# Loading the neighbourhood values by image rows of all four blocks instead of by blocks: a two-layer hybrid attention kernel

## The chip, the cores and the metric

One core of a Trainium2 chip runs the whole program. The metric is the time that the device takes for one execution, in microseconds (us). The core has a matrix engine (TensorE, in the profile PE, with PEld for its weight loads), VectorE (DVE), ScalarE (ACT), GpSimd (POOL) and SyncE (SP). SP computes nothing; it issues transfers between the device's memory and the on-chip memory, one after the other in the program's order. The transfers run on 16 DMA engines. The on-chip memory has 128 rows, called partitions.

## The reference

The model has two post-norm layers over 1024 latent tokens (an image of 16 rows of 64 columns) and 256 context tokens, 1024 wide, in float32. The change lies in the first layer's token mixer. It has four differential attention heads and eight neighbourhood heads of width 64. A neighbourhood head lets each latent token look at a window of 8 rows and 16 columns around it and at all context tokens:

```
row_start = jnp.clip(r - wr // 2, 0, rows - wr)
col_start = jnp.clip(cidx - wc // 2, 0, GRID_W - wc)
...
bias = rpb[:, roff[:, None, None], col_off[None, :, :]]
s_win = jnp.einsum('bhqd,bhqkd->bhqk', q_row, k_win).astype(jnp.float32) * scale + bias
s_ctx = jnp.einsum('bhqd,bhkd->bhqk', q_row, k_ctx).astype(jnp.float32) * scale
p = jax.nn.softmax(jnp.concatenate([s_win, s_ctx], -1), axis=-1).astype(v.dtype)
return (jnp.einsum('bhqk,bhqkd->bhqd', p[..., :nw], v_win)
        + jnp.einsum('bhqk,bhkd->bhqd', p[..., nw:], v_ctx))
```

Around it stand the input and output projections, a second attention layer of another kind, and two feed-forward blocks, which the change does not touch.

## The kernel before

The program runs its stages in order: the first projection (`qkv`, which writes queries, keys and values to device memory), the first attention (`attn0`), the output projection and feed-forward of layer 0, the second layer's attention, and its feed-forward. All run on one core.

`attn0` works through eight units: units 0 to 3 are the differential heads, units 4 to 7 two neighbourhood heads each. A neighbourhood unit has nine jobs: one for the context tokens, then, for each of four groups j of 16 image columns and each of the two heads (hh), one job. A job's queries are 256 tokens (16 rows by 16 columns, in two halves s); its keys are 16 image rows of a band of 32 columns that begins at c0 = 0, 8, 24 or 32. The 512 window keys are four blocks of 128: block rb holds image rows 4 rb to 4 rb + 3, 32 columns each.

A job is cut into steps, and a table by hand (`PATTERN`, line 42) says how many rounds after the job's start each step is recorded, one job starting per round. For neighbourhood jobs: scores (X), their maximum with the bias table added (TR, on VectorE, line 943), the exponentials (E), two memsets on GpSimd that blank the unused part (MS, lines 952 and 953, three rounds on), the scaling by the reciprocal of the sum (S, GpSimd, line 820, two rounds on), transposes (T4 and T2, PE, line 830), a split into two summands, the products with the values (A, PE, five rounds on), and the output (FC, FIN, VectorE line 998, five rounds on). Order within PE, ACT, DVE and POOL is the order of recording, and nothing overtakes.

Between the jobs, `na_hooks` (line 1101) records what is fetched: values by `na_values` (line 1007), bias tables by `na_table` (line 1021), and the add of the mask to a table by `na_mask` (line 1028, on GpSimd). Values of group 0 and four of the six tables of a unit are asked for during the last jobs of the unit before; the mask add of its first table is recorded before its last job. The queries and keys of the next unit (`attn_unit`: twelve loads `ks`, `qs`, `ql`) are asked for before the fourth job. All these go out on SP's one queue, in this order, together with the store of a finished unit (line 1002). Each transfer there also waits until the eighth one before it has landed, since eight completion counters are used in turn.

The values lie in device memory as `svb`, 1280 tokens by 8 heads by two summands by 64, that is 4 KB for each token; a unit's two heads take 1 KB of them. A tile `vs` (128 partitions, four blocks, two heads, 128 numbers) holds one group j; seven such tiles are used in turn. The partition of a key in its block is 32 times the row in the block plus the column in the band. Tables (`tab`) are loaded by a pair of transfers each, with a source whose outermost count is 8.

Of the kernel before, what the change touches and what calls it, by code (L numbers as in the profile page):

```python
# [80 lines left out]
class Kernel:  # L81
# [925 lines left out]
    def na_values(self, sb, u, j):  # L1007

        src = self.svb[:, (u - 4) * 2:(u - 3) * 2].rearrange("t h a d -> t (h a d)")
        if j < 0:  # L1010
            v = self.vs[u, "c"] = self.t(sb, [P, 2, 2, P], "vc", F32R, bufs=2)
            self.dma(v.rearrange("p t h d -> p t (h d)"), src[NX:T, :].rearrange("(t p) c -> p t c", p=P))
        else:
            c0 = (0, 8, 24, 32)[j]
            v = self.vs[u, j] = self.t(sb, [P, 4, 2, P], "vs", F32R, bufs=7)
            for rb in range(4):
                sr = src[rb * 256 + c0:rb * 256 + c0 + 1, :]
                self.dma(v[:, rb].rearrange("p h d -> p (h d)"),
                         bass.AP(sr.tensor, sr.offset, [[64 * 1024, 4], [1024, 32], [1, 256]]))

    def na_table(self, sb, u, hh, v):

# [1783 lines left out]
```

## Time and profile before

| | us |
|---|---|
| median of three timed runs | 3321.28 |
| lowest, highest | 3315.80, 3325.24 |
| profiled execution | 3321.84 |
| its span | 3320.1 |
| PE busy | 3053.2 |
| VectorE busy | 2430.5 |
| ScalarE busy | 1547.6 |
| GpSimd busy | 981.9 |

The busy times are of the whole span; stages with different limits lie behind them. The neighbourhood units take the stretch from about 620 to 890 us. Views of the trace can be asked for a stretch: the waits (which instruction of which engine waited for what), the instructions in order of time, and the busy time of each engine with the granted TensorE clock (1.00 is 2.4 GHz, 0.50 is 1.2 GHz), the mean busy share of the 16 DMA engines and the rate that they moved.

### The profile page before, as it was taken

The page shows a single profiled execution, that of the slowest core. Times are in us where ns is not written, and L with a number is a line of the kernel's source. Part 1 is how long each engine was busy: PE and PEld are TensorE (multiplying, and loading weights), DVE is VectorE, ACT ScalarE, POOL GpSimd, SP SyncE. Part 2 cuts the span into 40 slices and gives each one's busy share as a digit, 9 for nine tenths or more (in the row PEclk, how much of TensorE's full clock was granted, in tenths as well). Part 3 has the DMA queues.
Part 4 walks back from the last instruction along what each step waited for, and adds up shares of the span by engine and source line. Part 5 has one row for each costly group of instructions (what it writes and reads, how often), then busy time and mean ns, then how long its engine had stood idle before and what let it go on. Part 6 is the DMA issues. An engine that isn't in the chain of part 4 may idle for free.

```text
span 3320.1 us, 47807 instructions
## 1 busy us (share of the span) xinstructions
PE 3053.2 (92%) x17519; PEld 2708.8 (82%) x17519; DVE 2430.5 (73%) x4109; ACT 1547.6 (47%) x3186; POOL 981.9 (30%) x772
## 2 busy tenths in 40 slices
PE   7999989975888899889999999989999899999996
PEld 5999878874777899679999788768998788888875
DVE  5776669875778998588998654448887876665576
ACT  5344357775634444333544336137774433333443
POOL 1345445563543321131231002123543101111021
PEclk9999999997998999999999999989999999999998
DMA  7565564375524333644342444264423322225542
GB/s 229 160 214 192 174 173 104 96 170 152 166 82 134 108 115 102 178 144 123 108 140 89 150 154 170 89 221 117 96 69 111 108 83 83 89 81 182 179 134 89
DMA packets 369191, 444.67 MB, mean 134 GB/s; under 512 B 52430, under 2 KB 265071, under 8 KB 365499
## 3 DMA queue, kind: packets, MB, share of 16 engines
q1 hardware_dynamic: 367629, 438.44, 43.8%
q8 instruction: 138, 2.26, 0.3%
q0 software_dynamic: 848, 3.02, 0.3%
q14 instruction: 96, 0.79, 0.1%
q10 hardware_dynamic: 480, 0.16, 0.0%
HBM read 344.51 MB, written 98.18 MB: 133 GB/s over the span
## 4 chain that ended last, share of the span: by engine, by line
PE 43%; DVE 9%; issue 3%; ACT 2%; DMA 2%; POOL 0%; SPq 0%; ACTq 0%; DVEq 0%; POOLq 0%
PE pa L125 18%; PE pc L125 17%; PE xps L125 3%; DVE blk L1736 2%; PE ops L125 2%; PE b L830 2%; DVE big L1830 1%; PE b L125 1%; ACT eu L1327 1%; DVE big L2246 0%; DMA eh<-hm 0%; DVE pt L1835 0%; ACT blk L1733 0%; DVE eu L1414 0%; DVE r L1259 0%
## 5 line engine op out<-in xcount | busy, mean ns | idle before, releaser
L125 PE MATMUL pc<-u,blk 128*128 128x320 f32 (+1 forms) x3540 | 631.6, 335 | 24.3 <-DVE blk L1736 10.1
L125 PEld LDWEIGHTS pc<-u,blk 128*128 128x128 f32 x3540 | 571.3, 191 | 66.1 <-DVE blk L1736 12.5
L1733 ACT CAST blk<-big 128x512 fp32r<-128x512 f32 x311 | 190.1, 621 | 301.5 <-PE pc L125 115.1
L125 PE MATMUL pa<-blk,blk 128*128 128x512 f32 x1188 | 291.5, 396 | 18.8 <-DVE blk L1736 16.4
L1736 DVE TENSOR_TENSOR blk<-wf,blk 128x512 fp32r<-128x512 f32 x377 | 290.1, 772 | 7.1 <-ACT blk L1733 7.1
L125 PEld LDWEIGHTS pa<-blk,blk 128*128 128x128 f32 x1188 | 225.6, 191 | 73.0 <-issue 9.2
L1733 ACT CAST blk<-wf 128x512 fp32r<-128x512 f32 x377 | 232.1, 618 | 111.4 <-PE pc L125 59.8
L1736 DVE TENSOR_TENSOR blk<-big,blk 128x512 fp32r<-128x512 f32 x311 | 224.3, 721 | 57.7 <-ACT blk L1733 57.6
L125 PE MATMUL pa<-u,blk 128*128 128x320 f32 (+1 forms) x1356 | 241.3, 327 | 9.2 <-DVE pt L1835 8.3
L125 PE MATMUL ps<-uh,whl 128*128 128x320 f32 (+2 forms) x1024 | 233.8, 315 | 8.6 <-DVE whl L122 5.9
L125 PEld LDWEIGHTS pa<-u,blk 128*128 128x128 f32 x1356 | 215.5, 190 | 20.5 <-DVE pt L1835 9.0
L125 PE MATMUL pc<-blk,blk 128*128 128x512 f32 x924 | 219.6, 392 | 5.1 <-DVE blk L1736 5.0
L125 PE MATMUL pa<-big,ohl 128*128 128x512 f32 x756 | 201.8, 404 | 19.0 <-POOL ohl L122 4.8
L125 PEld LDWEIGHTS pc<-blk,blk 128*128 128x128 f32 x924 | 174.2, 189 | 42.2 <-ACT u L113 5.4
L247 POOL TENSOR_TENSOR macc<-mw,macc 128x512 f32<-128x512 f32 x96 | 149.5, 1559 | 172.1 <-ACT mw L244 92.2
L820 POOL TENSOR_SCALAR p<-p,rec 128x384 f32<-128x384 f32 (+1 forms) x160 | 143.5, 913 | 179.1 <-DVE rec L635 154.6
L125 PEld LDWEIGHTS pa<-big,ohl 128*128 128x128 f32 x756 | 145.9, 195 | 53.0 <-POOL ohl L122 9.6
L125 PEld LDWEIGHTS ps<-uh,whl 128*128 128x128 f32 x1024 | 176.1, 192 | 11.9 <-DVE whl L122 6.3
L603 ACT ACTIVATE p<-xps,nm 128x1024 f32<-128x1024 f32 x128 | 143.3, 1120 | 83.6 <-DVE nm L599 76.7
L624 DVE TENSOR_REDUCE mx<-xps 128x1 f32<-128x1024 f32 x128 | 156.0, 1219 | 22.2 <-PE xps L125 21.4
L125 PE MATMUL ps<-ul,whl 128*128 128x320 f32 (+2 forms) x512 | 160.7, 314 | 1.6 <-DVE ul L415 1.5
L1288 POOL TENSOR_TENSOR r<-r,rowg 128x1024 f32<-128x1024 f32 x28 | 74.2, 2650 | 296.1 <-ACT r L1277 147.2
(418 smaller groups left out, 6907.9 us busy)
## 6 DMA issues: line engine op xcount, KB each, us to landing
wf<-in_ffn_w_in SPq DMA_DIRECT2D x132, 512.0 KB
wf<-in_ffn_w_out SPq DMA_DIRECT2D x88, 512.0 KB
mw<-in_mod_w SPq DMA_DIRECT2D x64, 512.0 KB
wf<-in_mod_w SPq DMA_DIRECT2D x32, 512.0 KB
uhl<-sun SPq DMA_DIRECT2D x13, 1024.0 KB
wf<-in_ev_w_in SPq DMA_DIRECT2D x24, 512.0 KB
hid<-r SPq DMA_DIRECT2D x22, 512.0 KB
ks<-sk SPq DMA_DIRECT2D x32, 320.0 KB
```

Source lines behind the costliest of these rows:

```text
L125: self.nc.tensor.matmul(out, lhsT, rhs, start=start, stop=stop)
L247: nc.gpsimd.tensor_tensor(out=acc[n][:, conds - 1, :], in0=w, in1=acc[n][:, conds - 1, :], op=ALU.add)
L603: self.nc.scalar.activation(out=out, in_=in_, func=AF.Exp, scale=scale, bias=st["nm"][:, s:s + 1], accum_out=st["sums"][:, s, part:part + 1])
L624: nc.vector.tensor_reduce(out=st["mx"][:, s, 0:1], in_=st["x", s], axis=AX.X, op=ALU.max)
L820: self.nc.gpsimd.tensor_scalar(out=ap, in0=ap, scalar1=rec, scalar2=0.0, op0=ALU.mult, op1=ALU.add)
L830: nc.tensor.transpose(tp[:, b, s * P:(s + 1) * P], pt()[:, s, (k0 + b) * P:(k0 + b + 1) * P], self.ident)
L1288: eng.tensor_tensor(out=e["r"], in0=e["r"], in1=e["rows"]["g"], op=ALU.mult)
L1327: nc.scalar.activation(out=u[:, kt, :], in_=pt[:, kt, :], func=AF.Identity, scale=sc, bias=sh)
L1733: nc.scalar.copy(hi, src)
L1736: nc.vector.tensor_tensor(out=lo, in0=src, in1=hi, op=ALU.subtract)
L1830: eng.tensor_tensor(out=T[n], in0=x, in1=y, op=ALU.subtract)
```

## The change

The four loads that fill one `vs` tile are cut another way. Before, each load fills one block in all 128 partitions; its source is walked as 4 image rows, 32 columns, 256 numbers. Now each load fills the 32 partitions of one image row of a block, for all four blocks; its source is walked as 32 columns, 4 blocks, 256 numbers. The number of loads, their bytes (128 KB), the contiguous runs (1 KB) and the contents of the tile are the same.

```
         else:
             c0 = (0, 8, 24, 32)[j]
             v = self.vs[u, j] = self.t(sb, [P, 4, 2, P], "vs", F32R, bufs=7)
-            for rb in range(4):
-                sr = src[rb * 256 + c0:rb * 256 + c0 + 1, :]
-                self.dma(v[:, rb].rearrange("p h d -> p (h d)"),
-                         bass.AP(sr.tensor, sr.offset, [[64 * 1024, 4], [1024, 32], [1, 256]]))
+            for r in range(4):
+
+                sr = src[r * 64 + c0:r * 64 + c0 + 1, :]
+                self.dma(v[r * 32:(r + 1) * 32].rearrange("p b h d -> p b (h d)"),
+                         bass.AP(sr.tensor, sr.offset, [[1024, 32], [256 * 1024, 4], [1, 256]]))
```

On SP's queue this is the place where unit 5 asks for its last two value tiles, stores unit 4's output and asks for the first tables of unit 6 (`vs_1361` and `vs_1381` are unit 5's groups 2 and 3, `tab_1382` is unit 6's first table, `vc_1396` its context values; "x4" means four in a row, and the sizes are of the tile's side):

```order
-L109 DMA vs_1361_7585<-svb_41_116 128x1x256 x4
+L109 DMA vs_1361_7585<-svb_41_116 32x4x256 x4
 L1002 DMA so0_455_4201<-o5_1227_7042 128x1280
-L109 DMA vs_1381_7710<-svb_41_116 128x1x256 x4
+L109 DMA vs_1381_7710<-svb_41_116 32x4x256 x4
 L109 DMA tab_1382_7716<-rexp_167_805 128x1x384 x2
 L109 DMA vc_1396_7785<-svb_41_116 128x2x256
```

Nothing moved: the same sixteen loads for each unit stand at the same places, with another shape. On the other engines the order is the same too. What the first matmul on a `vs` tile waits for differs: it read one load's partitions and now reads a quarter of each of the four.

## Rows read from the trace of the kernel before

**Rows 1.** The page's first line.
```profile
span 3320.1 us, 47807 instructions
```
**Rows 2.** Waits, 690 to 850 us: waiter <- releaser: total us, times, longest.
```profile
POOL tab L1030 <- DMA tab<-rexp: 51.4, 5, 21.7
...
PE xps L830 <- POOL p L953: 44.9, 3, 20.1
```
**Rows 3.** GpSimd in order of time: start, us, engine, line, what, [idle before <- releaser].
```profile
695.56 1.26 POOL L777 TENSOR_TENSOR o<-o,rs_y 128x640 f32<-128x640 f32 x1
705.70 1.80 POOL L1030 TENSOR_TENSOR tab<-tab,namask 128x768 f32<-128x768 f32 x1 [8.88 <-DMA tab<-rexp]
...
747.11 1.83 POOL L820 TENSOR_SCALAR p<-p,rec 128x384 f32<-128x384 f32 x3 [1.86 <-DVE rec L635]
768.59 1.80 POOL L1030 TENSOR_TENSOR tab<-tab,namask 128x768 f32<-128x768 f32 x1 [19.65 <-DMA tab<-rexp]
...
805.48 1.82 POOL L820 TENSOR_SCALAR p<-p,rec 128x384 f32<-128x384 f32 x3 [1.86 <-DVE rec L635]
829.05 1.80 POOL L1030 TENSOR_TENSOR tab<-tab,namask 128x768 f32<-128x768 f32 x1 [21.74 <-DMA tab<-rexp]
...
887.98 0.60 POOL L1002 DMA_DIRECT2D so<-o  x1 [8.50 <-DVE o L998]
```
**Rows 4.** SP's queue in order of time, 680 to 870 us, same columns.
```profile
681.24 13.95 SPq L109 DMA_DIRECT2D vs<-svb  x8
695.30 2.36 SPq L109 DMA_DIRECT2D tab<-rexp  x2
...
743.35 5.75 SPq L109 DMA_DIRECT2D vs<-svb  x4
749.19 3.67 SPq L1002 DMA_DIRECT2D so<-o  x1
752.91 5.13 SPq L109 DMA_DIRECT2D vs<-svb  x4
758.13 2.66 SPq L109 DMA_DIRECT2D tab<-rexp  x2
...
813.75 4.80 SPq L109 DMA_DIRECT2D vs<-svb  x4
818.65 2.66 SPq L109 DMA_DIRECT2D tab<-rexp  x2
...
859.06 7.35 SPq L109 DMA_DIRECT2D u<-in_ev_w_out  x7
```
**Rows 5.** Stretches: length, busy us by engine (instructions), TensorE clock, DMA share, GB/s.
```profile
690.00:697.50 7.50, 5.66 (x46) 5.17 (x44) 7.33 (x25) 6.49 (x18) 4.87 (x8) 1.00 0.28 95
...
722.50:730.00 7.50, 6.58 (x55) 6.44 (x55) 6.57 (x20) 7.10 (x21) 2.70 (x7) 1.00 0.97 203
...
766.50:768.50 2.00, 0.00 (x0) 0.00 (x0) 0.00 (x0) 0.00 (x0) 0.00 (x0) 0.50 0.53 183
772.00:776.00 4.00, 4.00 (x25) 4.00 (x24) 1.65 (x2) 2.78 (x7) 4.00 (x7) 0.64 0.39 128
...
860.00:880.00 20.00, 18.36 (x147) 17.29 (x146) 18.45 (x52) 19.30 (x50) 12.02 (x28) 1.00 0.83 274
```
**Rows 6.** DMA issues by line: what, count in the program, size of each.
```profile
ks<-sk SPq DMA_DIRECT2D x32, 320.0 KB
...
tab<-rexp SPq DMA_DIRECT2D x48, 192.0 KB
...
vs<-svb SPq DMA_DIRECT2D x64, 128.0 KB
...
so<-o SPq DMA_DIRECT2D x7, 640.0 KB
...
vc<-svb SPq DMA_DIRECT2D x4, 256.0 KB
```
**Rows 7.** VectorE in order of time, unit 4's last addition into its output.
```profile
734.94 0.43 DVE L998 TENSOR_TENSOR o<-ops,otmp 64x256 f32<-64x256 f32 x1
```

## Prediction

> **What bounds the kernel now.** The profiled execution's span is 3320.1 us [rows 1] and its own time 3321.84 us; the median of the three timed runs, 3321.28 us, lies 0.56 us below that, so a sum made against the trace carries over to the median almost as it stands.
>
> The diff touches one thing, the 64 loads `vs<-svb` of 128 KB [rows 6], which SP issues in the neighbourhood half of the attention (units 4 to 7, about 620 to 886 us). I therefore read that stretch and not the page's shares. First the waits of 690 to 850 us [rows 2]: GpSimd waits 51.4 us for the tables `tab<-rexp`, five times, and PE waits 44.9 us in three pieces for a GpSimd memset (line 953). The second wait is the first one handed on: in GpSimd's order the add of the mask to a table stands ahead of the memset and the scaling of the probabilities of the jobs that are still running. GpSimd's own rows [rows 3] show the three waits that matter: 8.88 us before 705.70, 19.65 us before 768.59 and 21.74 us before 829.05, together 50.3 us. Each is the first mask add of the next unit (units 5, 6 and 7), and near the end of the second no engine computes at all (766.5 to 768.5) [rows 5].
>
> Why are the tables late? SP's rows [rows 4] show a queue that has fallen behind: the table pair of unit 6 goes out at 758.13, directly behind two groups of `vs` (743.35 and 752.91) and a store (749.19) that itself took 3.67 us to issue. The store was not waiting for its data, for the last addition into it (DVE line 998, the eighth of unit 4) began at 734.94 [rows 7]. So SP was some 14 us late with everything. And a `vs` group of four needs 5 to 7 us of SP (13.95 us for eight at 681.24).
>
> Then the transfer rate [rows 5]. From 690 to 697.5, while the eight `vs` of 681.24 drain, the 16 DMA engines are busy 0.28 of the time and move 95 GB/s. At the tail of a table load (766.5 to 768.5) the share is 0.53 at 183 GB/s; under the `ks`, `qs`, `ql` loads (722.5 to 730) it is 0.97 at 203 GB/s. That reads as four, eight and sixteen engines at work, and the outermost counts of the sources in the code are 4 for `vs` (blocks of rows), 8 for `tab`, and 64 for `ks`. A `vs` load is thus a queue of 32 KB on each of four engines, and what comes after it on SP's queue, table loads included, stands behind it on those four.
>
> A unit's prefetch can be added up as a serial queue: 16 `vs` at 131,072 B / 95 GB/s = 1.38 us are 22.1; 12 `ks`/`qs`/`ql` at 327,680 B / 203 GB/s = 1.61 are 19.4; 12 `tab` at 196,608 B / 183 GB/s = 1.07 are 12.9; one `vc` and one `so` at 203 GB/s are 1.3 and 3.2. The sum is 58.9 us; the distances between the three ends of waiting are 62.9 and 60.5 us [rows 3]. Computing a unit takes less: from 705.70 to the end of the scaling that began at 747.11 (748.9) are 43.2 us, from 768.59 to 807.3 are 38.7. So in units 5 and 6 the queue of loads is the bound, and each microsecond taken out of it moves the next end of waiting.
>
> **The change part by part.** It removes 64 loads that have 4 at the outermost place of the source and adds 64 of the same bytes, the same 1 KB runs and the same place in SP's order that have 32 there, on both sides. No instruction moves on any engine; one wait changes: the first matmul that reads a `vs` tile now waits for all four of its loads, since each brings a quarter of the partitions of every block, where it waited for one and its successors for the others. Its cover is the distance in the list of jobs: a job multiplies by `vs` five rounds after it starts, about half a unit, and the tile is asked for at the latest two jobs ahead. So I cost it at nothing; without that cover it would be three more transfers, about 2 us, per tile.
>
> *The price of a new load.* No row of before shows a load of 32 partitions with 1 KB runs and a step of 1 MB inside a partition. From one side it is bounded by the loads of 64 partitions: 203 GB/s, 0.65 us. From the other by the loads of 128 partitions (860 to 880): 274 GB/s at a share of 0.83, so 330 GB/s when busy, 0.40 us [rows 5]. Upwards there is no such nearby row; the old price, 1.38 us, is the point where nothing is gained. I take 0.57, nearer to the 64-partition rows: a group of four fills first one half of the partitions, then the other, so it behaves like those rows, with some overlap between the halves that those mostly lack.
>
> The Trainium skill bears on this. "SBUF — State Buffer", section "Door 1: The DMA port swizzle (why `[64,N]` ≈ `[32,N]`)", says that 32 partitions reach as many of the 16 memory ports as 64 do, eight, and 128 all of them. That fits the rows on 64 and 128 partitions; no run here shows 32 alone. By its figures (half of 435 GB/s, an estimate of 0.60 us) the sum below would be 31 us.
>
> *What of it lies on the path.* Between the start of the trouble and the issue of unit 7's first table at 818.65 stand ten groups of `vs`, that is 40 loads: eight at 681.24, the last four at 813.75 [rows 4]. All are in front of the table load that ends the third wait. 40 x (1.38 - 0.57) = 32.4 us. The stores' long issue (3.67 us at 749.19) is the same backlog seen from SP and is not counted again. The other 24 loads (unit 4's first two groups, unit 7's own, the tail) gain nothing, for no compute engine waits behind them for more than a microsecond, and none waits for `vs` itself.
>
> *What is late next.* The tables still. Unit 5's first lands 8 x 0.81 = 6.5 us earlier, so 2.4 of 8.88 us stay. Unit 6's lands 24 x 0.81 = 19.4 us earlier, at 749.2, and GpSimd now comes there at 748.9 - 6.5 = 742.4: 6.8 us stay of 19.65. Unit 7's lands at 829.05 - 32.4 = 796.7 and GpSimd comes at 749.2 + 38.7 = 787.9: 8.8 us stay of 21.74. That leaves 18.0 of 50.3 us, and the 32.3 us that go agree with the sum. Because waits stay, the computing between them is not the bound, and the half clock that follows each wait (0.64 granted on average from 772 to 776, with PE busy all 4.00 us, between the levels 1.2 and 2.4 GHz) gives nothing back in units 5 and 6; unit 7 may save up to 2 us if its wait gets short enough that the clock does not fall.
>
> From 829 on the kernel should run as before, only earlier: the stores and the first loads of the next stage stand behind `vs` in the same queue (`u<-in_ev_w_out`, 859.06, is issued 20 us before the last output of this stage leaves at 887.98), and they move with it.
>
> Sum: 3321.84 - 32.4, with a third of a microsecond to two for the clock and the gaps of 2 to 4 us per unit that the serial sum leaves open: about 3288 us, and the same on the scale of the median.
>
> **The rivals.**
>
> *A full cure.* If the new loads run at the 128-partition rate, 40 x 0.98 = 39 us go, and if with them the 2 to 4 us of gaps per unit go too (they may be four engines draining while twelve stand still), some 46: 3276 us. For it speaks that the sum of transfers is short of the measured period; against it that a quarter of the partitions is written at a time. All 50.3 us would need 0.12 us per load, out of reach.
>
> *A narrower target is slower.* From 128 to 64 partitions the busy rate fell from 330 to 203 GB/s; if 32 lose by the same ratio again it is 125 GB/s, 1.05 us, and 13 us go: 3309. If they lose half, 1.29 us, 4 us go: 3318, which no measurement would tell from 3321. A source step of 1 MB could do a part of the same: at 0.70 us, half way from 0.57 to the 0.82 at which the forecast ends, 27 us go, 3294. (The Trainium skill, "DMA: Bandwidth & Descriptors", section "Latency and other measured facts", has a row on row pitches at large powers of two: 207 GB/s at 512 KiB between partitions, 164 at 2 MiB, against 214 with a padded pitch. That speaks against the new source pattern; a rate between the two, 185 GB/s, would be an estimate of 0.71 us. No row of before has a step of 1 MB.)
>
> *It is not spread.* If the engines are handed out by another count than the outermost one, four engines keep the work, and the time stays at 3321. Against it stand the three shares 0.28, 0.53 and 0.97 for 4, 8 and 64.
>
> *Slower.* The new loads take all sixteen engines. While the old ones drain, engines 5 to 16 are free, and half of each table load passes there. If a new load needs more than 1.38 us (under 95 GB/s over sixteen engines), then it holds up everything, and no engine passes it. At half that rate, 2.76 us, 40 x 1.38 = 55 us are added to the same three waits: 3377. The point from which it decides is a run of 1 KB at 172 ns on each engine (1.38 us for eight runs); under the `ks` loads 1 KB takes 16 engines x 1024 B / 203 GB/s = 81 ns, so it would have to be over twice as slow as the slowest row near it.
>
> **How the numbers follow.** Forecast, 3288 with waits left (3299 at 0.82 us per load, 3277 at 0.40 with some of the gaps gone): 0.67. Full cure, below 3277: 0.05. A slower target or source, or a part given back later, 3299 to 3311: 0.16. Slower target by half, or not spread, 3311 to 3331: 0.08. Slower, over 3331: 0.04. A difference of 0.3%, 10 us, is about what a measurement of this kernel can tell from none. Faster by more than that: 0.67 + 0.05 + 0.15 = 0.87; same 0.09; slower 0.04. The range from 3273 to 3309 leaves out the two last cases, a part of the one before them and little below: about 0.17.
>
> **What would show it.** In the profile after: the DMA share while a `vs` group drains near 0.9 instead of 0.28, and SP's time for a group near 2 us instead of 5; the GpSimd waits for `tab<-rexp` down from 51.4 to some 18 us, with the first nearly gone and the second and third at 5 to 10; the ends of waiting some 47 to 50 us apart instead of 60 to 63; everything after about 890 us as long as before. It is wrong if `vs` groups still need 5 us of SP (not spread, or a slow target), if the table waits shrink but the kernel does not (another wait took over, as the stores that wait for DVE in SP's queue), or if the stage after 890 us has grown by what this one lost.

## Result: 38 us less, the table waits down from 50 to 18 us

| | before | after |
|---|---|---|
| median, us | 3322.89 | 3284.59 |
| lowest, highest, us | 3315.80, 3325.24 | 3282.58, 3290.26 |
| span of the profiled execution, us | 3320.1 | 3280.8 |

The ratio after/before is 0.9888 with a 95% interval of 0.9876 to 0.9900. The forecast was 3288 us, in a range of 3273 to 3309. (The median of before is now 3322.89 and not 3321.28, since it was timed again beside the changed kernel.)

First the waits of the changed kernel from 650 to 850 us (waiter <- releaser: total us, times, longest). The mask add is line 1031 now, and answers to line 1030 of [rows 2].

```profile
PE xps L830 <- POOL p L953: 12.8, 3, 6.4
POOL tab L1031 <- DMA tab<-rexp: 10.9, 3, 8.0
POOL tab L1031 <- DMA vs<-svb: 7.4, 1, 7.4
```

GpSimd's waits before its mask adds are 10.9 + 7.4 = 18.3 us where they were 51.4, and PE's wait for the memset behind them went with them, from 44.9 to 12.8. (The 7.4 us are put down to `vs`; the table pair stood right behind those loads in SP's queue, and in a second profile, below, the same wait is put down to the tables.) GpSimd in order of time, to be held against [rows 3]:

```profile
694.60 1.84 POOL L1031 TENSOR_TENSOR tab<-tab,namask 128x768 f32<-128x768 f32 x1 [2.65 <-DMA tab<-rexp]
...
743.74 1.80 POOL L1031 TENSOR_TENSOR tab<-tab,namask 128x768 f32<-128x768 f32 x1 [7.42 <-DMA vs<-svb]
...
790.26 1.80 POOL L1031 TENSOR_TENSOR tab<-tab,namask 128x768 f32<-128x768 f32 x1 [8.04 <-DMA tab<-rexp]
...
848.68 0.60 POOL L1002 DMA_DIRECT2D so<-o  x1 [8.50 <-DVE o L998]
```

The ends of waiting are 49.1 and 46.5 us apart instead of 62.9 and 60.5, and from the last of them to the store of unit 7 it is 58.4 us, nearly as before (58.9). SP's queue, against [rows 4]:

```profile
660.36 0.34 SPq L109 DMA_DIRECT2D so<-o  x1
...
675.80 10.65 SPq L109 DMA_DIRECT2D vs<-svb  x8
686.77 1.28 SPq L109 DMA_DIRECT2D tab<-rexp  x2
...
724.03 4.91 SPq L109 DMA_DIRECT2D vs<-svb  x4
730.22 0.34 SPq L1002 DMA_DIRECT2D so<-o  x1
731.78 3.50 SPq L109 DMA_DIRECT2D vs<-svb  x4
735.38 1.28 SPq L109 DMA_DIRECT2D tab<-rexp  x2
...
795.22 2.78 SPq L109 DMA_DIRECT2D vs<-svb  x4
...
802.26 1.83 SPq L109 DMA_DIRECT2D vs<-svb  x4
```

The store of unit 4 takes 0.34 us to issue instead of 3.67, the table pair behind it 1.28 instead of 2.66: the backlog is gone there. The stretches (length, busy us by engine with instructions, TensorE clock, DMA share, GB/s), of the changed kernel:

```profile
681.50:689.00 7.50, 5.88 (x44) 5.09 (x42) 7.39 (x24) 6.50 (x21) 4.15 (x10) 1.00 1.03 204
694.60:790.30 95.70, 76.62 (x578) 72.58 (x576) 77.00 (x214) 75.39 (x206) 58.96 (x101) 0.94 0.86 202
640.00:660.00 20.00, 15.44 (x116) 13.45 (x115) 17.99 (x28) 10.42 (x25) 15.78 (x8) 1.00 0.00 1
668.00:675.00 7.00, 5.77 (x45) 5.27 (x44) 6.36 (x20) 5.84 (x19) 5.25 (x11) 1.00 1.04 214
```

and of the kernel before from the end of its first wait to that of its third:

```profile
705.70:829.05 123.35, 77.74 (x566) 73.60 (x566) 73.92 (x204) 73.28 (x200) 59.06 (x101) 0.82 0.62 159
```

While eight value loads drain, the share is 1.03 at 204 GB/s, where it was 0.28 at 95 GB/s [rows 5]. (The share adds up the packets' times, so it can pass 1.00.) The stretch is not theirs alone: the last of the key and query loads passes in it, for eight value loads are 1.05 MB and 204 GB/s over 7.5 us are 1.53 MB. The packets from 685 to 688 us (number, MB, sizes; then the queue's own, with their share):

```profile
DMA packets 728, 0.68 MB, mean 227 GB/s; under 512 B 83, under 2 KB 726, under 8 KB 727
...
q1 hardware_dynamic: 727, 0.66, 109.9%
```

Without the 83 small ones the queue's packets are of 1 KB on average, that is, value loads alone: 0.66 MB in 3 us, 220 GB/s, 0.60 us for a load of 128 KB. Key and query loads alone, into 64 partitions, pass at 214 GB/s (the fourth line of the stretches). From the first to the third wait the engines are busy 0.86 of the time instead of 0.62. PE does the same work there (76.6 and 77.7 us), in 95.7 us instead of 123.4. The third line is for later: before the store that opens the stretch nothing at all is loaded for 20 us.

**Where the 38 us went.** From the SP store that opens the stretch to unit 7's store the stage takes 848.68 - 660.36 = 188.3 us; before it took 887.98 - 665.17 = 222.8 us:

```profile
665.17 0.32 SPq L109 DMA_DIRECT2D so<-o  x1
```

From there to the end are 2432.1 us in both. So 34.5 us of the 39.3 between the two spans lie in the stage; the other 4.8 lie ahead of it, where the kernels are the same. In the profiles of all kernels here (but the last, which moves that store) the opening lies between 660.4 and 667.2 us and the rest behind unit 7's store between 2428.8 and 2437.4, with no relation to the value loads that shows: executions differ by that much. A second profile of the changed kernel (below) gave 186.0 us for the stage, so its gain is 34 to 37 us.

### The profile page after: what moved, and what is told of

Its sections match the earlier page's. It is cut to its first block, busy times and chain, and to the rows that moved or that the text cites. A ratio compares the mean times of both kernels' runs of the same rounds, so it can differ in the third digit from the quotient of the medians.

```text
span 3280.8 us, 47823 instructions
## 1 busy us (share of the span) xinstructions
PE 3046.2 (93%) x17519; PEld 2705.4 (82%) x17519; DVE 2430.0 (74%) x4109; ACT 1547.0 (47%) x3186; POOL 981.7 (30%) x772
## 3 DMA queue, kind: packets, MB, share of 16 engines
q1 hardware_dynamic: 368397, 438.45, 44.9%
## 4 chain that ended last, share of the span: by engine, by line
PE 44%; DVE 8%; issue 2%; ACT 2%; DMA 2%; SPq 0%; POOL 0%; ACTq 0%; DVEq 0%; POOLq 0%
PE pc L125 18%; PE pa L125 18%; PE xps L125 3%; PE ops L125 2%; DVE blk L1737 2%; PE b L830 2%; PE b L125 1%; ACT eu L1328 1%; DVE big L1831 1%; SPq L109 0%; DVE big L2247 0%; DMA eh<-hm 0%; DMA v<-in_mla_w_ukv 0%; DVE eu L1415 0%; DMA uhl<-sun 0%
## 5 line engine op out<-in xcount | busy, mean ns | idle before, releaser
L125 PE MATMUL pc<-u,blk 128*128 128x320 f32 (+1 forms) x3540 | 629.4, 334 | 24.6 <-DVE blk L1737 10.6
```

Of the source, the lines that this page charges most:

```text
L125: self.nc.tensor.matmul(out, lhsT, rhs, start=start, stop=stop)
```

## Experiments

Every kernel was timed beside the kernel before on the same chip, and each ratio is to that one.

### The same kernel again

> The changed kernel once more. 3283 to 3290 us. In the first profile of it the store that frees SP's queue in unit 4 came 4.8 us earlier than in the profile of before, although no changed load precedes it by more than 45 us. If that is only a difference between executions, it comes at another time here (660 to 665 us) while the stretch from it to the last output of unit 7 is again about 188 us.

3284.68 us (3283.66 to 3285.73), ratio 0.9887 [0.9870, 0.9903]. The opening store came at 663.67 us, and the stage took 186.0. The waits are 2.18, 7.54 and 6.28 us, their ends at 697.45, 745.16 and 790.84. So 2 us is what the single waits differ by from execution to execution.

### The forty loads alone, and the twenty-four others alone

```
-            for r in range(4):
+            if (u, j) in [(4, 2), (4, 3)] or u in (5, 6):
+                for r in range(4):
...
+            else:
+                for rb in range(4):
...
```

The second kernel has the condition negated.

> New loads only for the ten groups (40 loads) that stand in SP's queue between unit 5's first table and unit 7's: units 5 and 6, and groups 2 and 3 of unit 4; the other 24 loads as before. My theory (only loads queued ahead of the table that ends the third wait count): the whole gain of the change, 3282 to 3290 us, GpSimd waits for tables of some 3, 7 and 8 us. Rival (every load gives its share of 38 us): 40 of 64, about 3299 us.

> The complement: new loads only for the 24 others (unit 4's groups 0 and 1, all of unit 7), the 40 as before. My theory: no gain, 3317 to 3326 us, GpSimd waits of some 9, 20 and 22 us. Rival (every load gives its share): 24 of 64 of 38 us, about 3308 us.

The forty alone give 3285.20 us, ratio 0.9889 [0.9875, 0.9904], all of the gain. The twenty-four others alone give 3322.91 us, 1.0008 [0.9998, 1.0017], nothing. Equal shares for every load (3299 and 3308 us) are excluded. GpSimd in the second kernel:

```profile
704.83 1.80 POOL L1037 TENSOR_TENSOR tab<-tab,namask 128x768 f32<-128x768 f32 x1 [8.57 <-DMA tab<-rexp]
767.49 1.80 POOL L1037 TENSOR_TENSOR tab<-tab,namask 128x768 f32<-128x768 f32 x1 [19.68 <-DMA tab<-rexp]
...
830.19 1.80 POOL L1037 TENSOR_TENSOR tab<-tab,namask 128x768 f32<-128x768 f32 x1 [23.58 <-DMA tab<-rexp]
```

Those are the three waits of [rows 3], to within 2 us. Which loads lie on the path was read rightly.

### Fewer engines, and smaller loads

Both kernels fill a tile with eight loads of 64 KB; they differ in the outermost count of the source, 2 in the first and 32 in the second, and in the partitions that a load fills, 64 and 32. The first edit is against the kernel before, the second against the changed one.

```
             for rb in range(4):
...
+                for r in (0, 2):
...
+                             bass.AP(sr.tensor, sr.offset, [[64 * 1024, 2], [1024, 32], [1, 256]]))
```

```
+                for b in (0, 2):
...
+                             bass.AP(sr.tensor, sr.offset, [[1024, 32], [256 * 1024, 2], [1, 256]]))
```

> Eight loads of 64 KB for a tile, each two image rows of one block: outermost count 2 in the source, 64 partitions, 1 KB runs. My theory (the outermost count is the number of engines that work): two engines, 47 GB/s, a share near 0.13 while only values drain, 11 us for a tile instead of 5.5; ten tiles on the path make 3370 to 3385 us. Rival (the gain came from the partitions or the pattern in memory, not from the engines): within 10 us of the kernel before.

> Eight loads of 64 KB for a tile, each one image row of two blocks: outermost count 32, 32 partitions, 1 KB runs. It differs from the run with outermost count 2 in nothing but that count and the partitions. My theory: sixteen engines, share near 1; SP issues twice as many loads at about 0.3 us each, which the transfer time of 0.3 us each still covers: 3283 to 3295 us. Rival (issue time or the eight transfers in flight bind): 3300 to 3315 us.

The first takes 3385.54 us, ratio 1.0190 [1.0174, 1.0206], the second 3301.52 us, 0.9935 [0.9921, 0.9950]. Of the first (outermost 2), the stretch in which 16 value loads drain:

```profile
690.00:696.00 6.00, 3.73 (x29) 3.24 (x28) 5.94 (x18) 4.97 (x15) 4.29 (x7) 1.00 0.14 47
```

and their issue on SP:

```profile
679.40 24.74 SPq L109 DMA_DIRECT2D vs<-svb  x16
```

Two stretches of the second (outermost 32) in which such loads drain:

```profile
687.00:690.00 3.00, 3.00 (x27) 3.00 (x26) 2.90 (x12) 2.97 (x8) 1.65 (x2) 1.00 0.50 116
689.90:692.70 2.80, 1.62 (x13) 1.37 (x12) 2.74 (x6) 2.34 (x8) 2.20 (x6) 1.00 0.46 139
```

and its SP in order of time:

```profile
677.40 15.29 SPq L109 DMA_DIRECT2D vs<-svb  x16
...
743.31 4.21 SPq L109 DMA_DIRECT2D vs<-svb  x8
```

and, from 689.9 to 692.7 us alone:

```profile
689.92 2.77 SPq L109 DMA_DIRECT2D vs<-svb  x6
```

At the same number of loads and the same bytes the outermost count makes 84 us. The shares of 0.14, 0.28, 0.53 and 1.03 at 47, 95, 183 and 204 GB/s stand beside outermost counts of 2, 4, 8 and 32: one engine for each, up to all sixteen. That is the mechanism of the change, and it is shown; the number of partitions is not its cause, for the key loads fill 64 too and pass at 214 GB/s. (The Trainium skill, "DMA: Bandwidth & Descriptors", section "Rules for kernel authors", says the same: an outermost dimension of fewer than 16 confines a transfer to at most that many engines. The trace agrees at 2, 4 and 8.)

The share counts engines and not bytes. For each engine those rates are 23.5, 23.8 and 22.9 GB/s at 2, 4 and 8, and 12.8 at 32 (13.8 at the 220 GB/s of value loads alone). So four times the engines gave 2.1 to 2.3 times the rate, and eight engines already move 183 GB/s, though that row is of table loads into 128 partitions. A value load with an outermost count of 8 was not tried.

The first kernel came out half a microsecond above the 3370 to 3385 us of its theory. The second went against my theory, which gave the number of loads no price, and into the range of its rival, issue time or the transfers in flight. Its three waits are 4.37, 12.96 and 15.09 us: forty more loads on the path at the same bytes cost 3301.52 - 3284.59 = 16.9 us, 0.42 us each. While they drain the share is only 0.46 to 0.50, and SP's shortest group of eight ahead of a late table takes 4.21 us, 0.53 us for each. The second stretch shows what sets that pace: six loads leave SP in 2.77 us, 0.46 us apart, and the engines move 139 GB/s, which is 64 KB in 0.47 us. So there the issue is the bound. (From 688 to 693 us SP waits 0.9 us for one landing and for nothing else.) A load of 128 KB drains in 0.60 us, longer than that.

### Every value load twice

```
+            v = self.vs[u, j] = self.t(sb, [P, 4, 2, P], "vs", F32R, bufs=5)
+            x = self.t(sb, [P, 4, 2, P], "vsx", F32R, bufs=2)
...
+                for d in (v, x):
...
```

> The changed kernel with every value load issued a second time, into a tile that nobody reads (five value tiles in turn instead of seven make the room). The price of a new load on the path, measured as a slope: 40 more loads at 0.6 us. My theory: 24 us more than the changed kernel, 3305 to 3312 us. Rival (the loads now hide beside the others, so another one costs little): under 3292 us.

3319.88 us, ratio 0.9996 [0.9986, 1.0005]; the waits are 8.20, 18.18 and 19.48 us. The forty added loads cost 35.3 us, 0.88 us each and not the 0.6 of the theory; the rival, under 3292 us, is further off. The tile's ring is also shorter here, five instead of seven, and may have a part in it; how the 0.88 us divide between bytes, issue and ring, no run shows. The drain rate's 0.60 us is what bytes cost that follow one another; a load that was added cost more.

### Tables asked for earlier, with the new loads and with the old

```
-            for v, hh, load, add in ((0, 0, (-1, 5), (-1, 8)), (0, 1, (-1, 6), (0, 0)), (1, 0, (-1, 7), (0, 1)),
+            for v, hh, load, add in ((0, 0, (-1, 2), (-1, 8)), (0, 1, (-1, 4), (0, 0)), (1, 0, (-1, 7), (0, 1)),
```

> The changed kernel with the first two tables of the next unit asked for earlier (before the third and the fifth job instead of before the sixth and the seventh), so that the first stands ahead of the twelve ks/qs/ql loads. My theory (the queue is still a few us longer than the computing of a unit): the waits move to the third table of each unit and shrink, since that is needed two rounds later: 10 to 16 us less than the changed kernel, 3268 to 3275 us. Rival (the remaining waits are set by the length of the queue whatever its order): 3280 to 3285 us.

> The kernel before with its old loads, and the first two tables of the next unit asked for earlier, as in the run on the changed kernel. My theory (the queue of a unit is 59 us long against some 40 of computing, so whatever stands last in it is late): the waits move to the third table, 5 to 15 us less than before, 3307 to 3317 us. Rival (the tables were only badly placed behind the values): nearly all of the 50 us of waiting goes, 3272 to 3285 us.

With the new loads 3284.76 us, ratio 0.9888 [0.9873, 0.9903], no gain; with the old ones 3318.90 us, 0.9989 [0.9979, 0.9998]. GpSimd with the new loads and early tables, unit 7:

```profile
791.78 1.80 POOL L1031 TENSOR_TENSOR tab<-tab,namask 128x768 f32<-128x768 f32 x1 [5.95 <-DMA tab<-rexp]
799.26 1.81 POOL L1031 TENSOR_TENSOR tab<-tab,namask 128x768 f32<-128x768 f32 x1 [3.58 <-DMA tab<-rexp]
804.26 1.83 POOL L1031 TENSOR_TENSOR tab<-tab,namask 128x768 f32<-128x768 f32 x1 [1.09 <-DMA tab<-rexp]
```

The wait of one table is spread over three, 10.6 us in all. With the new loads my theory's gain of 10 to 16 us did not come, and the rival's 3280 to 3285 us did. With the old ones nearly nothing was won, 2 us short of my theory's range, and the rival, that the tables were only badly placed (3272 to 3285 us), fell. In both, what is moved up makes another thing late, as a queue that is too long does. So the old loads' harm was not just their place ahead of the first two tables.

### Half of the keys and queries in another queue

What the changed kernel still waits for (18 us) was then the question. Here the loads of half 1 of units 5 to 7 are issued by GpSimd.

```
+                    if u > 4 and half:
+                        nc.gpsimd.dma_start(out=d[dst, m, :].bitcast(F32), in_=s.bitcast(F32))
```

> The kernel after, with one thing moved: for units 5 to 7 the six of a unit's twelve key and query loads that belong to its second half (320 KB each) are issued on GpSimd's queue instead of SP's; same bytes, same place in the order of recording. Theory (what still waits in the kernel after is SP's one queue, in which each load stands behind those before it): with six of twelve such loads in another queue the tables are issued and land earlier; the three waits before the first mask adds of units 5, 6 and 7 (in the kernel after 2.7, 7.4 and 8.0 us) fall to under 2 us each, GpSimd loses at most some us to issuing, and the time is 10 to 16 us under the kernel after, 3268 to 3276. Rival (the loads are bound by the engines and the half of the partitions that they write, whatever queue they stand in): the same bytes pass in the same time, the waits stay within 2 us of what they are and the time is 3281 to 3288. Second rival (GpSimd's place in the order decides): each issue on GpSimd stands ahead of its mask adds and scalings and waits for the queue's earlier loads; GpSimd's waits move there and the time is over 3290.

3283.41 us, ratio 0.9878 [0.9862, 0.9895]: not to be told from the changed kernel, as the first rival said. GpSimd:

```profile
698.77 1.81 POOL L1031 TENSOR_TENSOR tab<-tab,namask 128x768 f32<-128x768 f32 x1
...
746.51 1.80 POOL L1031 TENSOR_TENSOR tab<-tab,namask 128x768 f32<-128x768 f32 x1 [5.54 <-DMA tab<-rexp]
...
792.05 1.80 POOL L1031 TENSOR_TENSOR tab<-tab,namask 128x768 f32<-128x768 f32 x1 [6.47 <-DMA tab<-rexp]
```

The first wait is gone and nothing is won: the distances are 47.7 and 45.5 us, as in the changed kernel's second profile, and the first of these mask adds begins 34.4 us after the opening store where it was 34.2. GpSimd comes later, as it issues six loads itself (672.1 to 675.2 us in its row). From the first of these to the last the engines have a share of 0.87 at 207 GB/s. (The Trainium skill, "DMA: Bandwidth & Descriptors", section "Rules for kernel authors", says that two transfers to disjoint halves of the partitions share the engines whichever queue issues them, and advises one transfer into all 128 instead. The first part agrees with this run; the second is tried below.)

### Unit 4's loads ahead of the store, and whole keys

The 20 us without any transfer (share 0.00, above) lie ahead of the store at 660.36, for whose data SP waited 30.3 us (SP's waits of the changed kernel, 600 to 700 us; line 786 is the last step to unit 2's output; the second line is of 700 to 712 us, at unit 3's store):

```profile
SPq L109 <- ACT o L786: 32.6, 2, 30.3
...
SPq L109 <- ACT o L786: 2.3, 1, 2.3
```

(The expectation below calls the store at 660.36 unit 3's. It is unit 2's; unit 3's goes out at 707.12.)

The first kernel asks for unit 4's groups 2 and 3 and its last tables ahead of that store; the second, built on it, also loads the keys into all 128 partitions at once.

```
+                if u == 4 and j > 1:
+                    du, n = 0, 1
...
+                if u == 4 and v == 2:
+                    load = (0, 1)
```

```
...
+            self.dma(ks[:, m, :], self.sk[u][m].rearrange("h r t -> (h r) t"))
...
-                self.dma(ks[dst, m, :], self.sk[u][half, rows, :])
```

> The kernel after, with four requests of unit 4 moved up: its value groups 2 and 3 and its last table pair are asked for before unit 4's second job, so that on SP's queue they stand ahead of the store of unit 3 instead of behind it. In the kernel after that store waits 30.3 us for its data, and the DMA engines have a share of 0.00 from 640 to 660 us; the eight value loads (0.64 us each) and the pair (2 x 1.07 us) pass in that empty stretch. Theory (from the store on, the loads of units 5 to 7 are bound by the bytes that the engines pass, a share of 0.86 at 202 GB/s between the first and the third wait, so what counts is how much stands behind the store): 8 x 0.64 + 2.1 = about 7 us less to pass, the third wait ends that much earlier, and the time is 4 to 8 us under the kernel after, 3276 to 3281. Rival (what the loads wait for are buffers: the keys of unit 5 go where unit 3's were, and so on, each unit's loads starting when the one before has been scored): the queue's start does not matter and the time is 3283 to 3287.

> The kernel of e11_unit4_early, with the keys also kept in device memory in the order in which a tile holds them, so that one load of 640 KB fills all 128 partitions (two for each unit) where two of 320 KB filled 64 each; the stores of the keys are cut in two for it, eight units times two more in the projection stage. Theory (a load into half of the partitions passes at 203 GB/s, one into all at about 330): 2 x 2.0 us instead of 4 x 1.61 us, 2.5 us less for each unit, and units 5 to 7 give 5 to 8 us more than e11_unit4_early, that is 3268 to 3276. Rival (with the share of the engines already at 0.86, the rate does not rise with the partitions, or the added stores cost in the projection what is won here): within 2 us of e11_unit4_early, or slower.

The first takes 3285.61 us, ratio 0.9891 [0.9876, 0.9906]; the second 3290.42 us, 0.9902 [0.9885, 0.9918]. Neither theory held. The first kernel's time is in the range of its rival, that the loads wait for buffers, which the next section tests. Of the first, SP's waits from 670 to 830 us:

```profile
SPq L109 <- ACT o L786: 5.9, 1, 5.9
```

and SP in order of time:

```profile
700.57 1.22 SPq L109 DMA_DIRECT2D tab<-rexp  x2
708.95 0.34 SPq L109 DMA_DIRECT2D so<-o  x1
709.39 1.49 SPq L109 DMA_DIRECT2D tab<-rexp  x2
710.97 0.49 SPq L109 DMA_DIRECT2D ks<-sk  x1
```

Unit 5's last table pair goes out 36.2 us after the opening store (664.41 us here) where it was 42.0. What is won there is lost at the next store, unit 3's: SP stands 5.9 us for its data, and unit 6's keys go out behind it at 710.97, as in the changed kernel (709.19). That points to the stores in the same queue rather than to the loads or their buffers; the last experiment takes the stores away. Whole keys brought nothing: the mask adds of units 6 and 7 are 49.8 us apart instead of 46.5. While unit 7's keys and queries pass, the first kernel and then the second:

```profile
758.00:771.00 13.00, 12.67 (x104) 12.30 (x103) 12.60 (x38) 12.27 (x34) 8.05 (x17) 1.00 1.06 199
...
763.00:776.00 13.00, 12.75 (x102) 12.38 (x101) 12.06 (x35) 11.73 (x33) 6.80 (x13) 0.98 1.06 194
```

The rate of loads into 128 partitions in [rows 5], 330 GB/s when busy, is not had there, among query loads that still fill halves; why, is open. The second kernel also has more stores in the projection stage, and how much of its 4.8 us they are is not separated.

### The stores out of the way

This kernel is built on the one that asks for unit 4's loads early.

```
-        self.dma(self.so[u], ot)
+        (self.nc.gpsimd if u > 1 else self.nc.sync).dma_start(out=self.so[u], in_=ot)
...
+                    if u == NU - 1:
+                        nc.gpsimd.dma_start(out=self.so[u], in_=ot())
+                    else:
+                        self.late = lambda: nc.sync.dma_start(out=self.so[u], in_=ot())
...
+        for u in range(5, NU):
+            at(u, 8, lambda: self.late())
```

> The kernel of e11_unit4_early, with the stores of units 2 to 6 taken out of SP's way: those of units 2 and 3 go through GpSimd's queue at the same place in the order of recording, and those of units 4 to 6 stay on SP but are asked for before the ninth job of the next unit, behind the loads that they stood ahead of. In e11_unit4_early SP waited 5.9 us for the data of unit 3's store, at 708.95, and sent unit 6's key and query loads only behind it; so the 7 us won ahead of it were given back there. Theory (the pace of units 6 and 7 is set by the queue from that store on): unit 6's loads start 5 to 7 us earlier, the waits of 4.8 and 7.1 us before the first mask adds of units 6 and 7 shrink to 0 to 4, and the time is 4 to 9 us under e11_unit4_early and the kernel after, 3276 to 3281. Rival (unit 6's loads wait for their buffers, which unit 4 has just left, or the share of the engines at 0.85 leaves no room): the distances between the first mask adds stay at 46 to 47 us and the time is 3283 to 3287.

3278.03 us (3273.95 to 3280.51), ratio 0.9865 [0.9848, 0.9882], as its theory said. All its runs lie below all of the changed kernel's, 6.6 us by the medians, and 7.6 us below the kernel that it was built on: the fastest version here. GpSimd in order of time:

```profile
663.26 0.59 POOL L817 DMA_DIRECT2D so<-o  x1 [3.90 <-ACT o L786]
...
696.52 1.81 POOL L1034 TENSOR_TENSOR tab<-tab,namask 128x768 f32<-128x768 f32 x1
...
711.39 0.61 POOL L817 DMA_DIRECT2D so<-o  x1 [4.54 <-ACT o L786]
...
740.33 1.86 POOL L1034 TENSOR_TENSOR tab<-tab,namask 128x768 f32<-128x768 f32 x1
...
781.16 1.85 POOL L1034 TENSOR_TENSOR tab<-tab,namask 128x768 f32<-128x768 f32 x1 [1.51 <-DMA tab<-rexp]
...
841.11 0.61 POOL L1003 DMA_DIRECT2D so<-o  x1 [8.51 <-DVE o L998]
```

and SP:

```profile
702.89 0.49 SPq L109 DMA_DIRECT2D ks<-sk  x1
...
714.95 12.74 SPq L109 DMA_DIRECT2D vs<-svb  x8
727.95 1.28 SPq L109 DMA_DIRECT2D tab<-rexp  x2
```

Unit 6's keys go out at 702.89, 8.1 us earlier than in the kernel it was built on, so it was not buffers that had held them, and the table waits are 1.7 us in all. The mask adds are 43.8 and 40.8 us apart, about the computing of a unit that the prediction read as 43.2 and 38.7. The waiting for the data of units 2 and 3 has not gone: it is GpSimd's now, 3.90 and 4.54 us, and there no load stands behind it. So the 18 us that the change left were not a price of loads only: a queue of about the length of the computing started late, behind stores whose data were not there. Two groups of stores were moved together, on top of unit 4's loads, so how much each gives is not separated.

## Why the prediction was right

**The number of engines.** Right: shares 0.14, 0.28 and 1.03 for 2, 4 and 32 at the outermost place.

**Which loads count.** Right, forty and no others: 3285.20 us with those alone, 3322.91 with the rest alone. The one wait that the change altered, a matmul's for all four loads of its tile, costs nothing as forecast: from 640 to 900 us no matmul or weight load of the changed kernel waits for a `vs` load.

**The steps from wait to wait.** The forecast had the three ends of waiting come 6.5, then 12.9, then 13.0 us sooner after one another, 32.4 in all. From the opening store to the first end it was 40.5 us and is 34.2, 6.3 less; the two distances fell by 13.8 and 13.9. That is 34.0 us, or 0.85 us for a load where 0.81 was said. The waits left were given as 2.4, 6.8 and 8.8 and are 2.65, 7.42 and 8.04, their sum 18.1 against 18.0. The up to 2 us that unit 7 might save did not come: from the third wait to its store it is 58.4 us instead of 58.9.

**The price of a new load.** 0.57 us was taken; value loads alone drain at 220 GB/s, 0.60 us, as fast within 3% as the loads into 64 partitions (214 GB/s, 0.61 us). So the overlap between halves that I allowed for hardly shows, and the step of 1 MB costs nothing that shows. (The 203 GB/s that I read as the rate of key and query loads is of a stretch in which tables pass too: SP issues four of them just ahead of it, from 717.48 on; it is close all the same.) At 0.60 the sum is 31.2 us. The other 2.8 us of the 34.0 no run assigns; the gaps of the old queue, which I counted with a third of a microsecond to two, are the nearest guess.

That the result came so close is in part luck. Only the difference of two prices was tested, 0.81 us forecast and 0.85 found. Where a new load was added, it cost 0.88 us; if that holds for the forty, an old one cost 1.73, and both of my prices were too low by about as much. (The Trainium skill, "SBUF — State Buffer", section "Door 1: The DMA port swizzle (why `[64,N]` ≈ `[32,N]`)", has 32 partitions as fast as 64, which 220 beside 214 GB/s agrees with. The row on pitches of large powers of two in the Trainium skill, "DMA: Bandwidth & Descriptors", section "Latency and other measured facts", which the prediction weighed against the change, is about the step between partitions; here that is 4 KB, and the step of 1 MB lies inside a partition and shows no effect.)

**What was at fault.** SP's time for a group of four was to be near 2 us. From 690 to 800 it is 2.5 to 5.4, and only the group at 802.26 takes 1.83: SP still waits for the eighth load before, which may be a key load of 320 KB. So one of the prediction's signs of being wrong, groups that still need 5 us of SP, would have misled: the group at 724.03 takes 4.9 us though its loads are spread. And "the queue of loads is the bound" was half of it. It holds for the kernel before, but the prediction's serial sum has no place for the time when SP stands at a store; that shows only in the last experiments.

**The rivals.** A slower target, loads that are not spread, and loads that need more than the old 1.38 us are excluded by 204 GB/s at a share of 1.03. The full cure's 0.40 us was not reached by the loads; most of the waits it would have removed went with the last experiment. Behind the stage nothing was given back (2432.1 us in both), and the clock gave nothing that shows: PE's busy time for the stretch is 1.1 us less though the mean granted clock rose from 0.82 to 0.94.

The median fell by 38.3 us and the trace of the stage by 34.5 (36.8 in the second profile). The 2 to 4 us between are no more than executions differ by, and nothing here assigns them.

## What to carry to other kernels

Look at the DMA share while one kind of load drains. Here shares of a half, a quarter and an eighth went with sources that begin with a count of eight, four and two, and turning the pattern so that a long dimension stands outermost set all engines to work without another byte or instruction. Read the rate beside the share: it need not rise as far. Add a queue up as a series and hold the sum against the distance between waits; that tells which loads lie on the path before anything is built. When the loads are as fast as they get and waits are left, look for what the issuing queue itself waits for: a store that is not ready holds back every load behind it. Here three edits to the loads gave nothing, and the last of them with five stores moved as well gave 6.6 us.

## What was not expected

A load in a queue has a price apart from its bytes: halving the loads at the same bytes cost 0.42 us for each one added, with the engines at a share of about a half and SP 0.46 us from one issue to the next.

Three edits, tables asked for earlier, half of the keys and queries in another queue, and unit 4's loads ahead of the store, each gave nothing measurable (3283.41 to 3285.61 us against 3284.59); only when the stores moved as well did 6.6 us follow. A wait that disappears without the time moving can be a sign that a later point sets the pace, or that the waiter itself now comes later.

Keys loaded whole into 128 partitions were no faster than in halves (3290.42 us against 3285.61).
